# An encoder-layer kernel: the attention gates' columns join the paired product stage, two weight sums of each pair are made by adding transfers, and the last normalisation is reordered

## The chip, the core and the metric

The program runs on one core of a Trainium2 chip. Its engines are TensorE (PE: matmuls, with its weight loads shown as PEld), VectorE (DVE), ScalarE (ACT), GpSimd (POOL) and SyncE (SP), which mostly issues transfers. The metric is device time in microseconds (us) of one execution, the median over several runs; lower is better. TensorE's clock has two levels, 2.4 and 1.2 GHz; the profile gives the granted clock of a stretch as a share of the higher one.

## The reference, cut to what matters

One layer of a streaming encoder, fp32, for 512 prompt tokens and 64 sample tokens (576 in all), width 2048:

```python
ca, cb, cg, q, k, v, ag, mq, mg = split_in_proj(x @ w_in)     # 2048 -> 6144 columns
u = ca * sigmoid(cb)                                          # 8 x 128 channels
y = conv31(concat(left, u)) + conv_b                          # depthwise, 31 taps
conv_out = silu(layer_norm(y)) @ w_pw
att = chunk_attention(q, k, v, rel_table)                     # 4 heads x 128 ("self heads")
mem = memory_attention(mq, mem @ w_mem_kv)                    # 4 heads x 128 ("mem heads")
mix = concat([conv_out * silu(cg), att * silu(ag), mem * silu(mg)])
y = layer_norm(ALPHA * x + mix @ w_out)
```

The outputs are y, the new convolution state, and the new keys and values.

## The kernel before

Every fp32 product is made of three matmuls on rounded halves: a 128 x 1024 block of weights (512 KB, `wraw`) is split into `whi` (an ACT cast, L185) and `wlo` (a DVE subtraction, L186), and high*high, low*high and high*low are added up in PSUM. `stage_plan` lists the blocks in the order of their use; one block is one *stage*. `next_stage` calls `weights(i)`, which splits blocks up to two stages ahead and loads up to five ahead, from 14 buffers that raw, high and low blocks share. A stage of an ordinary column tile (`tileA`, results `accA`) is 48 matmuls of 288 columns, and a tile takes two stages.

The order of the work: the values V (`accB`), then the *product stage*, then per self head the column tiles K, Q and the gate AG, then the keys and values of the memory (16 steps over k, `mem_kv`), then per mem head the tiles MQ and MG, the upper half of the output product, the pointwise product of the convolution, and the lower half of the output product with the final layer norm.

The product stage takes column tiles in pairs. With token columns and weight rows each cut in two, a pair is computed by seven half-size products (Strassen-like) of 24 matmuls of 288 columns, instead of the 2 x 2 x 48 matmuls of two ordinary tiles. Three of the seven weight operands are raw quarters (a11, a22, a12) and four are sums (s1 to s4), made by DVE adds of 128 x 1024 (L176, L178). Results `st` go to `pos` and `neg` through ACT copies and DVE adds. There are 12 pairs: eight for the convolution's inputs and four for its gate CG, which is spilled to DRAM (`cgd`) and read back late.

Side work runs between stages. After each stage `pump(ntaps, steps)` takes `steps` steps of the generators in `side` (an attention head advances from one `yield` to the next: scores, transposes, product with V, gating) and `ntaps` taps of the convolution, one DVE instruction of 128 x 606 each (L435). The whole program's order on each engine is fixed by the order in which this code issues; the numbers that steer it are `TAP_RATE`, `TAP_RATE_KV`, `TAP_RATE_OUT` and `TAPS_OF_PRODUCT`.

A self head's steps on PE: scores (`sA` to `sD`, L695 to L698), then, after softmax on DVE and ACT (L708 to L732), transposes of the probabilities into `pt` (L737, L745; later L756 to L760), and the product with V (`so`, `sos`). For a mem head: `msc`, `mpt` (L621, L629), `mo` (L637 to L639).

The convolution's norm (`conv_ln`): column sums `mean`, squares, `var` (L892), then a diagonal of factors `dg` and its spread `ra`, `rb` (L906, L907).

At the end the last 512 output columns are computed token tile by token tile (t = 4, 0, 1, 2, 3). `settle` adds the accumulator to the residual `z` (L1086) and takes statistics; for n < 3 it also multiplies z by the gain on POOL (L1089). `finish_stats` makes row factors `lncc` on POOL (L1052 to L1062); `finish_pe` transposes them (`cT`, L1068) and makes the four corrections `t` (L1075), which DVE applies (L1078) and SP writes out.

Of the kernel before, what the change touches and what calls it, by code (L numbers as in the profile page):

```python
# [21 lines left out]
H = 4  # L22
# [16 lines left out]
TAP_RATE = 4  # L39
TAP_RATE_KV = 0  # L40
TAP_RATE_OUT = 5
TAPS_OF_PRODUCT = (1, 1, 0, 1, 1, 1, 1)
WARM = 8
CONV_PAIRS = [(C_CA + j * P, C_CB + j * P) for j in range(NCB)]
GATE_PAIRS = [(C_CG + j * P, C_CG + (j + 1) * P) for j in range(0, NCB, 2)]
PAIRS = CONV_PAIRS + GATE_PAIRS
AHEAD = 5

# [6 lines left out]
def stage_plan():  # L55
# [21 lines left out]
    for h in range(H):  # L77
        for c in (C_K, C_Q, C_AG):
            col(c + h * P)
# [30 lines left out]
def hymba_kernel(ctx: ExitStack, tc: tile.TileContext, wst, xT, memT, xp, xs, kcT, vc, mkcT, mvc, biasx,  # L110
# [47 lines left out]

    def w_load(i):
        if i < len(plan):  # L160
            for b in item_blocks(plan[i]):
                w_fetch(b)

    def w_source(it):
        if it[0] == "P":
            return w_fetch(it[1])
        n, form = it[1:]
        q = quads(PAIRS[n])
        if form[0] == "a":
            return w_fetch(q[form])  # L170
        if form == "s3":
            return sum3.pop(n)
        a21 = w_fetch(q["a21"])
        if form == "s1":
            sum3[n] = wtile("wsum")
            nc.vector.tensor_add(sum3[n], w_fetch(q["a11"]), a21)  # L176
        other = w_fetch(q[{"s1": "a22", "s2": "a11", "s4": "a12"}[form]])
        nc.vector.tensor_add(a21, a21, other)  # L178
        return a21

    def w_split(i):
        if i < len(plan) and i not in whi:
            src = w_source(plan[i])
# [5 lines left out]
    def weights(i):  # L189
        for j in range(i, i + 3):  # L190
            w_split(j)
        for j in range(i + 3, i + AHEAD + 1):
            w_load(j)
        return whi[i], wlo[i]
# [212 lines left out]
    cg_dram = [dram([P, NT], "cgd") for _ in range(NCB)]  # L407
# [8 lines left out]
    def queue_conv(j):  # L416
# [22 lines left out]
        def last():  # L439
            t = TAPS - 1  # L440
            y = t5([P, NT], "y")
# [54 lines left out]
    def gate_sink(d1, d2):  # L496
        def second(neg, b0):
# [3 lines left out]
            nc.gpsimd.dma_start(d2, neg.rearrange("p a b -> p (a b)"))  # L501

        def both(c1, neg):
            nc.scalar.activation(c1, c1, AF.Silu)
            nc.gpsimd.dma_start(d1, c1.rearrange("p a b -> p (a b)"))
        return second, both

    def strassen(sinks):
# [3 lines left out]
        for sink in sinks + [None]:  # L512
# [14 lines left out]
            if not sink:  # L527
# [17 lines left out]
             + [gate_sink(cg_dram[j], cg_dram[j + 1]) for j in range(0, NCB, 2)])  # L545
# [27 lines left out]
    def mem_attn(h, qh, ql, qs, gate_ref):  # L573
# [41 lines left out]
        yield  # L615
# [27 lines left out]
        gate = gate_ref[0]  # L643
# [32 lines left out]
    def self_attn(h, qh, ql, qs, kh, kl, k, gref):  # L676
# [102 lines left out]
        nc.tensor.matmul(os_[:, :64], vs[:64, hs], TS[:64, 256:320], start=False, stop=True)  # L779
        yield  # L780
        gate = gref[0]
# [4 lines left out]
    def self_block(h):  # L786
        k = evac2(tileA(xrhs, 2, TAP_RATE), "k")
# [6 lines left out]
        qh, ql, qs = evac_q(tileA(xrhs, 2, TAP_RATE))  # L794
        gref = [None]
        side.append(self_attn(h, qh, ql, qs, kh, kl, k, gref))
        gref[0] = evac_act(tileA(xrhs, 2, TAP_RATE), "ag", AF.Silu)
# [56 lines left out]
    def mem_block(h):  # L854
        qh, ql, qs = evac_q(tileA(xrhs, 2, TAP_RATE, 2))
        gref = [None]
        side.append(mem_attn(h, qh, ql, qs, gref))
        gref[0] = evac_act(tileA(xrhs, 2, TAP_RATE, 2), "mg", AF.Silu)
# [124 lines left out]
    for n in range(4):  # L983
        accs, sacc = tileB(mlhs2, range(4), msl, list(range(8, 16)), ntaps=TAP_RATE_OUT, before=late_mix, steps=2)
# [15 lines left out]
    def load_cg(j):  # L1000
        scg.append(t6([P, 2, HALF], "cg"))
        nc.sync.dma_start(scg[j].rearrange("p a b -> p (a b)"), cg_dram[j])
# [88 lines left out]
    def scale_g(t, n, g):  # L1091
        rows = P if t < 4 else NS_TOK
        nc.vector.tensor_mul(z[t, n][:rows], z[t, n][:rows], g[:rows])

    g = load_g(0)
    for n in range(3):
        accs, sacc = tileB(mlhs2, range(4), msl, list(range(8)))
        g2 = load_g(n + 1)
        for t in range(4):
            settle(t, n, accs[t], g)  # L1100
        settle(4, n, sacc, g)
# [20 lines left out]
    for t in (4, 0, 1, 2, 3):  # L1122
        todo = []
        for s in range(4):
            if t in (1, 2, 3) and due and (s == 3 or len(due) > 1):
                todo += finish_pe(*due.pop(0))
            part(t, s, held[s])
        settle(t, 3, accs[t], g, False)
        aggr, *rest = finish_stats(t)
        due.append((t, *rest))  # L1130
        with tc.issue_after(aggr.ins):
            for f in todo:
                f()
            scale_g(t, 3, g)
# [72 lines left out]
```

## Time and profile before

| what | value |
|---|---|
| median of 3 runs | 978.58 us (977.07 to 978.63) |
| profiled execution | 976.83 us, span 975.1 us |
| PE / DVE / ACT / POOL busy | 955.7 / 718.7 / 387.5 / 60.0 us |
| mean granted clock | 0.99 |
| V until 58.9 us, product stage until about 327 us | seven products to a pair |
| self heads until about 504 us, memory keys and values until about 545 us | |
| mem heads, upper half of the output, norm of the convolution at 740 us | |
| last matmul of the output product ends about 963.2 us | span ends at 975.1 us |

A busy PE here is a PE whose matmuls overlap each other: a row's mean duration (about 295 ns for 288 columns) is longer than the spacing of two matmuls. What a matmul costs is read from the chain of waits, as a stretch divided by its count.

### The profile page before, as it was taken

To read this page: it belongs to the slowest core of one execution; us is meant where nothing else is said; L and a number is where in the kernel's file an instruction comes from. 1 tells how busy PE (TensorE), PEld (TensorE's weight loads), DVE (VectorE), ACT (ScalarE), POOL (GpSimd) and SP (SyncE) were. 2 spreads that over 40 slices of the span, in tenths; PEclk is the share of its full clock that TensorE was granted. 3 is DMA by queue.
4 is the path that set the end of the run, shared out by engine and by line. 5 is a ranking of instruction groups with operands and counts; after the bars stand their busy time and mean duration, and the time that the engine had idled before them with its cause. 6 is when DMAs were issued, how large, how long until landed. Compare 5 with 4: busy or idle time off the path is not lost.

```text
span 975.1 us, 15245 instructions
## 1 busy us (share of the span) xinstructions
PE 955.7 (98%) x6133; PEld 881.4 (90%) x6133; DVE 718.7 (74%) x995; ACT 387.5 (40%) x667; POOL 60.0 (6%) x119
## 2 busy tenths in 40 slices
PE   9999999999999999999999999999998999999986
PEld 6899999999999999999988999989887889988864
DVE  7976998799868979898975543885988534635566
ACT  7654344443444425252537343455425313411200
POOL 0020000000000000000000000000000000012251
PEclk9999999999999999999999999999999999999987
DMA  8453333333444633333246542323354244322205
GB/s 320 143 170 113 114 104 119 127 100 101 152 138 149 231 112 124 105 101 126 78 131 191 192 137 88 111 66 110 119 193 156 75 134 135 109 80 85 76 7 187
DMA packets 44632, 124.58 MB, mean 128 GB/s; under 512 B 5710, under 2 KB 10318, under 8 KB 44562
## 3 DMA queue, kind: packets, MB, share of 16 engines
q1 hardware_dynamic: 40594, 109.88, 34.8%
q0 software_dynamic: 3680, 13.21, 3.6%
q8 instruction: 48, 0.79, 0.3%
q10 hardware_dynamic: 288, 0.52, 0.2%
q14 instruction: 22, 0.18, 0.1%
HBM read 106.72 MB, written 16.88 MB: 127 GB/s over the span
## 4 chain that ended last, share of the span: by engine, by line
PE 93%; DVE 4%; DMA 1%; ACT 1%; issue 1%; POOL 0%; DVEq 0%; SPq 0%; POOLq 0%; ACTq 0%
PE accA L234 32%; PE st L472 27%; PE accB L264 6%; PE accB L262 6%; PE accB L263 6%; PE accS L267 2%; PE accS L268 2%; PE mvacc L824 1%; PE accB L1113 1%; PE mvacc L826 1%; PE mkacc L830 1%; PE mkacc L831 1%; DVE z L1086 1%; PE mkacc L829 1%; PE accB L1114 1%
## 5 line engine op out<-in xcount | busy, mean ns | idle before, releaser
L186 DVE TENSOR_TENSOR wlo<-wraw,whi 128x1024 fp32r<-128x1024 f32 x175 | 217.7, 1247 | 175.3 <-PE accA L234 52.9
L185 ACT CAST whi<-wraw 128x1024 fp32r<-128x1024 f32 x175 | 183.2, 1050 | 296.2 <-DVE wlo L186 183.3
L234 PE MATMUL accA<-x,whi 128*128 128x288 f32 x1280 | 224.4, 297 | 0.0
L435 DVE SCALAR_TENSOR_TENSOR acc<-up,cw_sb,acc 128x606 f32<-128x606 f32 x232 | 196.6, 847 | 4.6
L234 PEld LDWEIGHTS accA<-x,whi 128*128 128x128 f32 x1280 | 187.8, 189 | 2.4 <-issue 1.5
L472 PE MATMUL st<-x,whi 128*128 128x288 f32 x768 | 153.5, 294 | 0.0
L234 PE MATMUL accA<-x,wlo 128*128 128x288 f32 x640 | 137.1, 296 | 0.0
L472 PEld LDWEIGHTS st<-x,whi 128*128 128x128 f32 x768 | 123.0, 188 | 0.3 <-ACT neg L538 0.2
L472 PE MATMUL st<-x,wlo 128*128 128x288 f32 x384 | 113.1, 295 | 0.0
L234 PEld LDWEIGHTS accA<-x,wlo 128*128 128x128 f32 x640 | 103.0, 189 | 0.0
L262 PE MATMUL accB<-whi,mix 128*128 128x512 f32 x224 | 89.1, 398 | 0.0
L264 PE MATMUL accB<-wlo,mix 128*128 128x512 f32 x224 | 88.4, 395 | 0.0
L263 PE MATMUL accB<-whi,mix 128*128 128x512 f32 x224 | 88.1, 393 | 0.0
L472 PEld LDWEIGHTS st<-x,wlo 128*128 128x128 f32 x384 | 72.0, 188 | 0.0
L472 PE MATMUL st<-t13h,wlo 128*128 128x288 f32 x192 | 56.6, 295 | 0.0
L472 PE MATMUL st<-t13l,whi 128*128 128x288 f32 x192 | 56.6, 295 | 0.0
L472 PE MATMUL st<-t13h,whi 128*128 128x288 f32 x192 | 56.5, 294 | 0.0
L264 PEld LDWEIGHTS accB<-wlo,mix 128*128 128x128 f32 x224 | 42.3, 189 | 9.8
L262 PEld LDWEIGHTS accB<-whi,mix 128*128 128x128 f32 x224 | 42.5, 190 | 9.3
L263 PEld LDWEIGHTS accB<-whi,mix 128*128 128x128 f32 x224 | 42.6, 190 | 9.2
L234 PE MATMUL accA<-sx,whi 128*128 128x288 f32 x256 | 44.5, 296 | 0.0
L178 DVE TENSOR_TENSOR wraw<-wraw,wraw 128x1024 f32<-128x1024 f32 x36 | 43.9, 1219 | 0.2
(331 smaller groups left out, 1486.0 us busy)
## 6 DMA issues: line engine op xcount, KB each, us to landing
wraw<-in_wst_dram SPq DMA_DIRECT2D x151, 512.0 KB, 3.6
xraw<-in_xT_dram SPq DMA_DIRECT2D x19, 288.0 KB, 4.5
z<-in_xp_dram SPq DMA_DIRECT2D x16, 256.0 KB, 4.6
out_y_dram<-z SPq DMA_DIRECT2D x16, 256.0 KB, 2.1
upd<-up POOLq DMA_DIRECT2D x8, 318.0 KB, 4.7
up<-upd SPq DMA_DIRECT2D x8, 318.0 KB, 4.0
yd<-y POOLq DMA_DIRECT2D x8, 288.0 KB, 2.8
y<-yd SPq DMA_DIRECT2D x8, 288.0 KB, 5.6
```

What stands on the lines that cost most here:

```text
L178: nc.vector.tensor_add(a21, a21, other)
L185: nc.scalar.copy(hi, src)
L186: nc.vector.tensor_sub(lo, src, hi.bitcast(F32))
L234: nc.tensor.matmul(acc[:, :HALF], stat[:, ws], mv[:, c], start=ki == 0 and pi == 0, stop=ki == len(klist) - 1 and pi == 2)
L262: nc.tensor.matmul(acc, lh, hi[:, ws], start=st, stop=False)
L263: nc.tensor.matmul(acc, ll, hi[:, ws], start=False, stop=False)
L264: nc.tensor.matmul(acc, lh, lo[:, ws], start=False, stop=en)
L267: nc.tensor.matmul(sacc, ss, hi[:, ws], start=st, stop=False)
L268: nc.tensor.matmul(sacc, ss, lo[:, ws], start=False, stop=en)
L435: nc.vector.scalar_tensor_tensor(acc[0], up[0][:, t:t + ACCW], cw_sb[:, j, t:t + 1], acc[0], op0=ALU.mult, op1=ALU.add)
L472: nc.tensor.matmul(acc[:, :HALF], stat[:, ws], mv, start=first and k == 0 and i == 0, stop=k == 7 and i == 2, skip_group_check=not first)
L824: nc.tensor.matmul(mvacc[t], mh[:, ts], hi[:, 512:], start=st, stop=False)
```

## The change

There are six parts.

1. The four gate tiles of the self heads (AG) leave the heads and become two more pairs of the product stage (14 pairs, 336 `st` matmuls more, 384 `accA` matmuls fewer). All gate pairs are spilled to DRAM from ACT's queue (before, from POOL's), and a self head reads its gate back after its product with V is issued.
2. Of the four weight sums of a pair, s1 and s3 are made by transfers. s3 is an ACT copy of a11 to which a POOL-issued transfer adds a21; s1 is the loaded a21 to which such a transfer adds a22. Both are started with the load of s1's stage, which now happens seven stages ahead instead of five (`AHEAD_PAIRS`). s2 and s4 stay DVE adds.
3. The taps are spread otherwise: ten to a pair instead of six, two (instead of four) after a self head's stage, one after two memory steps, three (instead of four) after a mem head's stage. The finished `y` of a channel block takes a buffer of the other pool (`t6`).
4. Each self head has four stages instead of six, with two steps of side work after each tile's stages instead of one. In the order, 48 `accA` matmuls stand between a head's scores and its first transposes (before, 96), 48 between the first and the second transposes, none between these and the product with V (before, 48). Head 3's steps lie among the memory steps, as before. A mem head loses one `yield`: the product `mo` follows `mpt` directly (before, 48 matmuls lay between).
5. In the upper half of the output product three steps are taken after a stage instead of two; `ra` comes behind nine more `accB` matmuls.
6. At the end, for n = 2 the multiplication with the gain is taken out of `settle`. POOL does it for n = 2 and for some tiles of n = 3 in the last loop, DVE for the others. `finish_pe` comes at other places: 64 `accB` matmuls stand ahead of the first `cT` (before, 40), and two tiles are finished after the last `accB` matmul (before, one).

```diff
-TAP_RATE = 4
-TAP_RATE_KV = 0
+TAP_RATE = 2
+TAP_RATE_KV = 1
+TAP_RATE_MEM = 3
...
-TAPS_OF_PRODUCT = (1, 1, 0, 1, 1, 1, 1)
+TAPS_OF_PRODUCT = (2, 1, 1, 2, 1, 1, 2)
...
-GATE_PAIRS = [(C_CG + j * P, C_CG + (j + 1) * P) for j in range(0, NCB, 2)]
+GATE_PAIRS = [(c + j * P, c + (j + 1) * P) for c, n in ((C_CG, NCB), (C_AG, H)) for j in range(0, n, 2)]
...
+AHEAD_PAIRS = 7
...
-        for c in (C_K, C_Q, C_AG):
+        for c in (C_K, C_Q):
...
+    def w_add(dst, b):
+        nc.gpsimd.dma_start(dst, wst[where[b]], accum_op=ALU.add)
+
...
-        if i < len(plan):
-            for b in item_blocks(plan[i]):
-                w_fetch(b)
+        if i >= len(plan):
+            return
+        for b in item_blocks(plan[i]):
+            w_fetch(b)
+        if plan[i][2:] == ("s1",) and plan[i][1] not in sum3:
+            n = plan[i][1]
+            q = quads(PAIRS[n])
+            sum3[n] = wtile("wsum")
+            nc.scalar.copy(sum3[n], w_fetch(q["a11"]))
+            w_add(sum3[n], q["a21"])
+            w_add(w_fetch(q["a21"]), q["a22"])
...
-            return sum3.pop(n)
+            return sum3[n]
...
-        if form == "s1":
-            sum3[n] = wtile("wsum")
-            nc.vector.tensor_add(sum3[n], w_fetch(q["a11"]), a21)
-        other = w_fetch(q[{"s1": "a22", "s2": "a11", "s4": "a12"}[form]])
-        nc.vector.tensor_add(a21, a21, other)
+        if form != "s1":
+            nc.vector.tensor_add(a21, a21, w_fetch(q[{"s2": "a11", "s4": "a12"}[form]]))
...
+            w_load(i)
...
-        for j in range(i + 3, i + AHEAD + 1):
-            w_load(j)
+        for j in range(i + 3, i + AHEAD_PAIRS + 1):
+            if j < len(plan) and (j <= i + AHEAD or plan[j][0] == "S"):
+                w_load(j)
...
-    cg_dram = [dram([P, NT], "cgd") for _ in range(NCB)]
+    gate_dram = {c: dram([P, NT], "gated") for pair in GATE_PAIRS for c in pair}
...
-            y = t5([P, NT], "y")
+            y = t6([P, NT], "y")
...
-            nc.gpsimd.dma_start(d2, neg.rearrange("p a b -> p (a b)"))
+            nc.scalar.dma_start(d2, neg.rearrange("p a b -> p (a b)"))
...
-            nc.gpsimd.dma_start(d1, c1.rearrange("p a b -> p (a b)"))
+            nc.scalar.dma_start(d1, c1.rearrange("p a b -> p (a b)"))
...
-             + [gate_sink(cg_dram[j], cg_dram[j + 1]) for j in range(0, NCB, 2)])
+             + [gate_sink(gate_dram[c], gate_dram[d]) for c, d in GATE_PAIRS])
...
-    def mem_attn(h, qh, ql, qs, gate_ref):
+    def load_gate(c):
+        g = t5([P, 2, HALF], "gate")
+        nc.sync.dma_start(g.rearrange("p a b -> p (a b)"), gate_dram[c])
+        return g
+
+    def mem_attn(h, qh, ql, qs, gref):
...
-        yield
...
-        gate = gate_ref[0]
+        gate = gref[0]
...
-    def self_attn(h, qh, ql, qs, kh, kl, k, gref):
+    def self_attn(h, qh, ql, qs, kh, kl, k):
...
-        yield
-        gate = gref[0]
+        gate = load_gate(C_AG + h * P)
+        yield
...
-        k = evac2(tileA(xrhs, 2, TAP_RATE), "k")
+        k = evac2(tileA(xrhs, 2, TAP_RATE, 2), "k")
...
-        qh, ql, qs = evac_q(tileA(xrhs, 2, TAP_RATE))
-        gref = [None]
-        side.append(self_attn(h, qh, ql, qs, kh, kl, k, gref))
-        gref[0] = evac_act(tileA(xrhs, 2, TAP_RATE), "ag", AF.Silu)
+        qh, ql, qs = evac_q(tileA(xrhs, 2, TAP_RATE, 2))
+        side.append(self_attn(h, qh, ql, qs, kh, kl, k))
...
-        qh, ql, qs = evac_q(tileA(xrhs, 2, TAP_RATE, 2))
+        qh, ql, qs = evac_q(tileA(xrhs, 2, TAP_RATE_MEM, 2))
...
-        gref[0] = evac_act(tileA(xrhs, 2, TAP_RATE, 2), "mg", AF.Silu)
+        gref[0] = evac_act(tileA(xrhs, 2, TAP_RATE_MEM, 2), "mg", AF.Silu)
...
-        accs, sacc = tileB(mlhs2, range(4), msl, list(range(8, 16)), ntaps=TAP_RATE_OUT, before=late_mix, steps=2)
+        accs, sacc = tileB(mlhs2, range(4), msl, list(range(8, 16)), ntaps=TAP_RATE_OUT, before=late_mix, steps=3)
...
-        nc.sync.dma_start(scg[j].rearrange("p a b -> p (a b)"), cg_dram[j])
+        nc.sync.dma_start(scg[j].rearrange("p a b -> p (a b)"), gate_dram[C_CG + j * P])
...
-    def scale_g(t, n, g):
-        rows = P if t < 4 else NS_TOK
-        nc.vector.tensor_mul(z[t, n][:rows], z[t, n][:rows], g[:rows])
-
...
-            settle(t, n, accs[t], g)
-        settle(4, n, sacc, g)
+            settle(t, n, accs[t], g, n < 2)
+        settle(4, n, sacc, g, n < 2)
+        gs = (g, g2)
...
-            if t in (1, 2, 3) and due and (s == 3 or len(due) > 1):
+            part(t, s, held[s])
+            if due and t > 1 and s == 2:
...
-            part(t, s, held[s])
+        if t == 1:
+            todo += finish_pe(*due.pop(0))
...
+        rows = P if t < 4 else NS_TOK
+        for n in (2, 3):
+            if t != 3 and (n == 2 or t in (4, 0)):
+                nc.gpsimd.tensor_mul(z[t, n][:rows], z[t, n][:rows], gs[n - 2][:rows])
...
-            scale_g(t, 3, g)
+            for n in (2, 3):
+                if t == 3 or (n == 3 and t in (1, 2)):
+                    nc.vector.tensor_mul(z[t, n][:rows], z[t, n][:rows], gs[n - 2][:rows])
...

```

On PE, self head 0: the last transposes of the probabilities (`pt` from `pA`, `pB`, `pS`) and what follows, before:

```order
L756 MATMUL pt_550_4190<-ident,pB_3933 128x128
L756 MATMUL pt_550_4190<-ident,pA_3932 128x128
L758 MATMUL pt_550_4190<-ident,pS_3934 128x64 x4
L760 MATMUL pt_551_4197<-ident,pS_3934 64x64
L234 MATMUL accA_4134<-x_91,whi_4047 128x288
L234 MATMUL accA_4135<-x_91,whi_4047 128x288
```

and now:

```order
L772 MATMUL pt_596_4595<-ident,pB_4412 128x128
L772 MATMUL pt_596_4595<-ident,pA_4411 128x128
L774 MATMUL pt_596_4595<-ident,pS_4413 128x64 x4
L776 MATMUL pt_597_4602<-ident,pS_4413 64x64
L789 MATMUL so_4610<-pT_583_4516,vw_4080 128x512
L790 MATMUL so_4610<-pL_584_4517,vw_4080 128x512
L791 MATMUL so_4610<-pT_583_4516,vw_4080 128x512
L789 MATMUL so_4610<-pT_586_4525,vw_4085 128x384
```

The product with V (`so`) now stands right behind the transposes, where the next column tile stood.

On PE, at the norm of the convolution, in the output product: `var` and `ra`, before:

```order
L268 MATMUL accS_7562<-wlo_7605,mixsamp_7346 128x512
L892 MATMUL var_7760<-ones,s_1051_7661 128x1 x4
L892 MATMUL var_7760<-ones,s_1051_7661 64x1
L906 MATMUL ra_7777<-dg_7771,ones 128x128 x4
L907 MATMUL rb_7778<-dg_7771,ones 128x64
L262 MATMUL accB_7813<-whi_7676,mix_7326 128x512
```

and now:

```order
L280 MATMUL accS_7806<-wlo_7697,mixsamp_7349 128x512
L906 MATMUL var_7841<-ones,s_1077_7753 128x1 x4
L906 MATMUL var_7841<-ones,s_1077_7753 64x1
L274 MATMUL accB_7802<-whi_7807,mix_7363 128x512
L275 MATMUL accB_7802<-whi_7807,mix_7363 128x512
L276 MATMUL accB_7802<-wlo_7808,mix_7363 128x512
L274 MATMUL accB_7803<-whi_7807,mix_7363 128x512
L275 MATMUL accB_7803<-whi_7807,mix_7363 128x512
L276 MATMUL accB_7803<-wlo_7808,mix_7363 128x512
L274 MATMUL accB_7804<-whi_7807,mix_7363 128x512
L275 MATMUL accB_7804<-whi_7807,mix_7363 128x512
L276 MATMUL accB_7804<-wlo_7808,mix_7363 128x512
L920 MATMUL ra_7858<-dg_7852,ones 128x128 x4
```

Nine matmuls of the output product moved between the two.

On POOL, early in the product stage (its other work there is a memset and the spill `upd` of each pair's `up`), before:

```order
L398 DMA vd_138<-v_649 64x512
L485 MEMSET up_941 128x30
L491 DMA upd_660<-up_941 128x636
L485 MEMSET up_1180 128x30
L491 DMA upd_661<-up_1180 128x636
L485 MEMSET up_1416 128x30
```

and now:

```order
L410 DMA vd_138<-v_652 64x512
L162 DMA wsum_733<-in_wst_dram 128x1024
L162 DMA wraw_729<-in_wst_dram 128x1024
L497 MEMSET up_947 128x30
L162 DMA wraw_960<-in_wst_dram 128x1024
L503 DMA upd_663<-up_947 128x636
L162 DMA wsum_964<-in_wst_dram 128x1024
L497 MEMSET up_1191 128x30
L162 DMA wsum_1208<-in_wst_dram 128x1024
L503 DMA upd_664<-up_1191 128x636
```

The rows of L162 are the adding transfers; two of them to a pair now stand among the spills in POOL's queue.

## Rows read from the trace of the kernel before

**Rows 1.** Page: engine, busy us (share) xinstructions; then the chain by engine.

```profile
PE 955.7 (98%) x6133; PEld 881.4 (90%) x6133; DVE 718.7 (74%) x995; ACT 387.5 (40%) x667; POOL 60.0 (6%) x119
...
PE 93%; DVE 4%; DMA 1%; ACT 1%; issue 1%; POOL 0%; DVEq 0%; SPq 0%; POOLq 0%; ACTq 0%
```

**Rows 2.** Waits of PE: line, releaser: us in total, times, longest.

```profile
PE cT L1068 <- POOL lncc L1056: 2.9, 1, 2.9
PE cT L1068 <- POOL lncc L1062: 2.5, 1, 2.5
PE ra L906 <- DVE dg L901: 2.5, 1, 2.5
PE mvacc L826 <- DVE ml L819: 1.5, 1, 1.5
PE mpt L621 <- ACT mp L612: 1.3, 1, 1.3
```

**Rows 3.** Chain of waits, two stretches: start us, us, what.

```profile
58.93 216.16 PE st L472 x1632
...
367.62 12.98 PE accA L234 x96
380.60 0.44 PE pt L737 x4
```

**Rows 4.** Stretches: us, busy of PE, PEld, DVE, ACT, POOL (xcount), PEclk, DMA.

```profile
193.00:215.00 22.00, 22.00 (x168) 22.00 (x167) 21.81 (x28) 8.10 (x14) 0.68 (x2) 1.00 0.36 111
```

**Rows 5.** Product stage by form: busy us, mean ns, idle before, releasers.

```profile
L186 DVE TENSOR_TENSOR wlo<-wraw,whi 128x1024 fp32r<-128x1024 f32 x71 | 86.2, 1222 | 34.5 <-PE st L472 17.7 <-ACT whi L185 16.4
L435 DVE SCALAR_TENSOR_TENSOR acc<-up,cw_sb,acc 128x606 f32<-128x606 f32 x64 | 54.2, 846 | 0.7
L178 DVE TENSOR_TENSOR wraw<-wraw,wraw 128x1024 f32<-128x1024 f32 x34 | 41.4, 1219 | 0.2
```

**Rows 6.** DMA issues: queue, count, KB each, median us to landing.

```profile
wraw<-in_wst_dram SPq DMA_DIRECT2D x151, 512.0 KB, 3.6
upd<-up POOLq DMA_DIRECT2D x8, 318.0 KB, 4.7
```

**Rows 7.** Timeline after self head 0's scores: start us, us, engine, line.

```profile
373.36 0.76 ACT L724 ACTIVATE pS<-pS,mx 64x576 f32<-64x576 f32 x1
374.03 1.23 DVE L186 TENSOR_TENSOR wlo<-wraw,whi 128x1024 fp32r<-128x1024 f32 x1
375.29 1.05 ACT L185 CAST whi<-wraw 128x1024 fp32r<-128x1024 f32 x1 [1.07 <-DVE wlo L186]
376.25 0.72 ACT L731 ACTIVATE pA<-pA,sm 128x512 f32<-128x512 f32 x1
377.67 0.49 ACT L731 ACTIVATE pB<-pB,sm 128x256 f32<-128x256 f32 x1
```

**Rows 8.** Timeline at mem head 0's transposes.

```profile
588.99 0.33 PE L629 MATMUL mpt<-ident,mps 64*128 64x64 f32 x2
590.17 0.57 ACT L624 CAST mph<-mpt 128x512 fp32r<-128x512 f32 x1
590.77 0.69 DVE L625 TENSOR_TENSOR mpl<-mpt,mph 128x512 fp32r<-128x512 f32 x1 [0.81 <-ACT mph L624]
```

**Rows 9.** Timeline of PE at three places, then DVE at the end.

```profile
745.82 0.63 PE L263 MATMUL accB<-whi,mix 128*128 128x512 f32 x1
747.10 0.63 PE L263 MATMUL accB<-whi,mix 128*128 128x512 f32 x1
...
939.39 0.63 PE L1114 MATMUL accB<-whi,mix 128*128 128x512 f32 x1
941.96 0.59 PE L1114 MATMUL accB<-whi,mix 128*128 128x512 f32 x1
...
963.28 0.69 DVE L1086 TENSOR_TENSOR z<-accB,z 128x512 f32<-128x512 f32 x1 [2.11 <-PE accB L1115]
964.91 2.65 DVE L1078 SCALAR_TENSOR_TENSOR z<-z,lnmv,t 128x512 f32<-128x512 f32 x4
```

## The prediction

> **What bounds the kernel now.** I read the page's busy times and its chain by engine first, then PE's waits, then the chain in two stretches for the price of a matmul, then single places. PE is busy 955.7 us and is 93% of the chain that ended last [rows 1]; only five of its waits are above 1.2 us, together 10.7 us [rows 2]. So the time is PE's work plus its few stalls. In the product stage DVE is nearly as full: 21.81 of 22 us, with PE busy for all 22 [rows 4]. The reader should see two different covers. In the product stage DVE has almost no room, and PE still never waits. In the heads DVE and ACT have room, but a softmax is a chain, hidden by the matmuls that stand between its steps. The change takes matmuls from the second place.
>
> **The change part by part.** All sums are made against the profiled execution, 976.83 us (1.7 us around its span of 975.1), which is 1.75 us under the median of 978.58.
>
> *PE's own work.* A product matmul costs 216.16/1632 = 0.1325 us, an attention-stage matmul 12.98/96 = 0.1352 us [rows 3]. 336 are added (44.5 us) and 384 go (51.9 us): -7.4 us. This is the only work removed from PE.
>
> *Weight sums.* DVE loses 20 adds of 1219 ns in all, s1 and s3 of 12 pairs against two more pairs of two, and gets more taps to a pair. A convolution pair now holds seven splits (8.6), two adds (2.4), three result adds of half the size of a 128x1024 add or less (1.8 at most), ten taps (8.5) and about 1 us of inputs: 22.3 us or a little less [rows 5], against 168 x 0.1325 = 22.25 us of PE. That is as full as before, when PE had no wait [rows 4]; I take 0. From the other side: where it is over by 5% for eight pairs, 9 us.
> The adding transfers are not in this trace. A plain 512 KB load takes 3.6 us, a POOL-issued 318 KB spill 4.7 [rows 6]. Worked from these, an adding transfer takes between 3.6 us and, at the spill's rate and with its destination read as well, 2 x 4.7 x 512/318 = 15.1 us. It is started about six stages before its sum is split, 6 x 24 x 0.1325 = 19 us. Hence 0, and I take the value near the spill, 7.6 us; at the upper end it still fits, with 4 us left for a plain load. What hides it is that lead; without it each pair would pay the excess.
> On this path the rows show POOL's spill landing within 4.7 us while DVE is 99% busy [rows 4, 6], and PE without a wait. The Trainium skill ("SBUF — State Buffer", SBUF: two separate sides, the "DVE blocks DMA" trap) says that a transfer issued from GpSimd's queue can be starved of its descriptors while VectorE holds the port the two share. By that rule 28 more transfers from this queue are the risk of the change, and it is the third rival below. The trace agrees with it only so far that POOL's spill is slower for its size than SP's load.
>
> *Self heads.* In head 0 the scores end at 367.62. Now 48 matmuls follow, not 96, so PE asks for the scaled probabilities at 367.62 + 48 x 0.1352 = 374.1. DVE's split runs from 374.03, and it waits for the end of those same 48 matmuls; ACT's weight cast waits for it, 375.29 to 376.3; only then come the scales, the last needed one ending at 377.67 + 0.49 = 378.2 [rows 7]. The order on ACT and DVE is the same after the change (exponentials, cast, scales; split, reciprocal), and what covered it was 96 matmuls, to 380.60 [rows 3]. Cost 4.0 us. In head 1 the reciprocal stands ahead of the split and no cast is between; the scales take 376.25 to 378.16 = 1.9 us after exponentials that end at 374.1 [rows 7], or about 1 us earlier since no taps are there: between 0.9 and 2.2, I take 1.2. In head 2 several tap instructions and a split stand ahead of the reciprocal: between 1.2 and 4.2 us, I take 3.0, nearer to head 0, whose order it shares. The product with V now follows the second transposes at once; six of its matmuls use the first transposes, so only the copy of the second can be late: 0 to 0.6 us a head, taken 0.3. Sum: 9.1 us.
>
> *Memory keys and values.* Before, their start waited 1.5 us for DVE, which had head 3's softmax in hand [rows 2]. That softmax now comes four steps later: -1.5 us. But DVE then has taps ahead of the first operands: from 0 to four taps and a split, 4 x 0.846 + 1.222 = 4.6 us [rows 5]. I take 0, since a whole softmax ahead of the operand cost only 1.5 us before.
>
> *Mem heads.* The transposes end at 588.99 + 0.33 = 589.3; the last low part ends at 590.77 + 0.69 = 591.5 [rows 8]. Four of the six `mo` matmuls fit between (0.94 us at 0.235, which is 0.1325 x 512/288), so 1.2 us is bare where ACT's weight cast stands between the two copies (heads 0 and 1), about half that in the other two: 3.6 us in sum; bounds 0 and 4.8. One tap less in each stage lets ACT's scales come earlier, and of the old wait of 1.3 us at `mpt` [rows 2] I count 0.8 as gone.
>
> *Norm of the convolution.* Nine matmuls (9 x 0.235 = 2.1 us) now stand in the wait of 2.5 us [rows 2]: -2.1. Behind that wait PE ran at its lower clock: from 745.82 to 747.10 a 512-column matmul took 0.43 us [rows 9]. Six such at 0.19 us too much: -1.2.
>
> *The end.* The first `cT` waited 2.9 us [rows 2]; 24 more matmuls (5.6 us) now stand ahead of it: -2.9. Eight matmuls behind it ran at 0.43 us, (941.96 - 939.39)/6 [rows 9]: -1.5. A second stretch of this kind later, behind eight small matmuls, I count half: -0.8. Against it, after the last matmul two tiles are finished instead of one: four more corrections, 2.65 us [rows 9]; `cT`'s own wait of 2.5 us [rows 2] stays. Balance -2.6 us. The gain's multiplications on POOL lie beside matmuls.
>
> *Sum.* Gains 7.4 + 1.5 + 0.8 + 3.3 + 2.6 = 15.6; losses 9.1 + 3.6 = 12.7; balance -2.9: 973.9 us for the profiled execution, 975.7 us as a median. So four fifths of the gain are given back in the heads.
>
> **The rivals.**
> *The covers hold.* The chains of the heads may run earlier than on before's clock, since DVE has no taps in heads 0 and 1 and ACT no gate and fewer table loads. For: DVE waits for PE at these places already [rows 7]. Against: it is this wait for PE that doesn't move. If 2 us of stalls are left, 965 us.
> *The heads' stalls whole, and the clock with them.* All at their upper bounds: head 1 +1.0, head 2 +1.2, products with V +0.9, mem heads +1.2, memory start +4.6 = 8.9 us more, and a low-clock stretch of 1.5 us behind the three longest. The trace has such stretches behind waits of 2.5 and 2.9 us and none behind those of 1.3 and 1.5 us [rows 2, 9]; head 0's 4.0 is longer than either. Together 989; a likely part of it, 983. This is the slower side: it decides once the stalls of the heads exceed 12.7 + 4.9 = 17.6 us.
> *The product stage slips.* POOL's adding transfers or DVE's 22.3 us a pair come last there. From 1 us a pair it costs 14 us: 990 or more. Against: the lead of 19 us.
> *Nothing of note.* The gate read-back or POOL's gain multiplications eat the small balance: 977 to 980.
>
> **How the numbers follow.** The forecast has 0.42, and its own range is 971 to 980.5; the covers hold 0.20; the stalls whole 0.27; the product stage 0.07; nothing of note 0.04. What a measurement of this kernel can tell from no change is 0.2%, 2 us, so faster is below 976.6 and slower above 980.5. Faster: 0.24 of the forecast's 0.42 plus 0.20 = 0.44. Within: 0.15 + 0.04 = 0.19. Slower: 0.03 + 0.27 + 0.07 = 0.37. The range of 8 in 10 goes from 965 to 988, over most of both rivals.
>
> **What would show it.** PE's busy time falls by some 7 us if the first term is right. PE's waits should list the first transposes of heads 0 and 2 (3 to 4 us each, on ACT's scales), `mo` on DVE's or ACT's copies, and no longer `ra` or the first `cT`. The product stage should end close to two pairs later, 44.5 us, with no wait of `st`. The time after the last matmul of the output product should grow from 12 to about 14.5 us. The forecast is wrong if the heads show no waits, if `st` waits for `wsum`, or if the clock falls in the heads.

## The result, and the profile after

The changed kernel takes 995.81 us (994.32 to 997.06, 4 runs) beside 977.83 us of the kernel before on the same chip: a ratio of 1.0179, 95% interval 1.0167 to 1.0191. It is slower by 18 us, where I had forecast 975.7 us in a range of 965 to 988. Its span is 994.1 us against 975.1, at a mean clock of 0.984.

The page of the changed kernel, busy times (compare [rows 1]) and transfers issued by POOL (compare [rows 6]; queue, count, KB each, median us to landing):

```profile
PE 957.4 (96%) x6085; PEld 878.5 (88%) x6085; DVE 700.0 (70%) x986; ACT 402.4 (40%) x685; POOL 81.1 (8%) x140
...
wsum<-in_wst_dram POOLq DMA_DIRECT2D x14, 512.0 KB, 8.2
wraw<-in_wst_dram POOLq DMA_DIRECT2D x14, 512.0 KB, 6.9
...
upd<-up POOLq DMA_DIRECT2D x8, 318.0 KB, 7.4
```

PE's busy time has not fallen by 7 us, though 48 matmuls are gone; it has risen by 1.7 us. The adding transfers (`wsum`, and `wraw` on POOL's queue) land after 8.2 and 6.9 us, close to the 7.6 I had taken. The page's chain of waits covers little of this execution, so I go by PE's waits and by stretches instead.

PE's waits after the change, to compare with [rows 2] (line, releaser: us in total, times, longest; some short ones and those ahead of the product stage are left out):

```profile
PE mvacc L838 <- ACT mh L832: 5.1, 2, 4.6
PE pt L753 <- ACT pA L747: 4.9, 2, 3.6
PE pt L753 <- issue: 3.7, 1, 3.7
PE mo L654 <- DVE mpl L641: 2.0, 6, 0.7
PE st L484 <- ACT neg L550: 1.8, 2, 1.1
PE mpt L637 <- ACT mp L629: 1.3, 1, 1.3
PE pt L776 <- DVE pL L767: 1.3, 1, 1.3
PE ra L920 <- DVE dg L915: 1.1, 1, 1.1
PE pt L772 <- DVE pL L757: 1.0, 1, 1.0
PE cT L1082 <- POOL lncc L1076: 0.2, 1, 0.2
```

The first wait of `cT` (2.9) and more than half of that of `ra` are gone, as forecast; so is nearly all of the last `cT`'s (2.5), which I had kept in the sum. New are `pt` in the self heads (3.7, 3.6, 1.3 us in heads 0, 2 and 1, and 2.3 us in head 3), `mo` and `st`; the wait at the first memory step (`mvacc`) has grown from 1.5 to 4.6 us.

Head 0's wait as a timeline (start us, us, engine, line; the last number is the engine's idle time before):

```profile
417.01 1.23 DVE L197 TENSOR_TENSOR wlo<-wraw,whi 128x1024 fp32r<-128x1024 f32 x1 [3.51 <-PE accA L246]
418.26 1.04 ACT L196 CAST whi<-wraw 128x1024 fp32r<-128x1024 f32 x1 [1.68 <-DVE wlo L197]
419.21 0.72 ACT L747 ACTIVATE pA<-pA,sm 128x512 f32<-128x512 f32 x1
420.83 0.30 PE L753 MATMUL pt<-ident,pA 128*128 128x128 f32 x1 [3.65 <-issue]
```

The split (L197) begins when the 48 matmuls end, ACT's weight cast follows it, and only then come the scales (L747) that the transposes need.

Now both kernels by stretch: product stage; self heads with memory keys and values; mem heads up to the end of their last `mpt`. (The memory steps of the kernel before end at 560.3 us, not at about 545 as the table ahead of the prediction has it.) Columns are length, busy time (and instructions) of PE, PEld, DVE, ACT and POOL, then granted clock, DMA share and GB/s. Before:

```profile
58.90:327.10 268.20, 268.20 (x2025) 268.01 (x2024) 226.31 (x259) 116.65 (x182) 14.82 (x35) 1.00 0.42 138
327.10:560.30 233.20, 231.40 (x1647) 220.68 (x1646) 189.97 (x280) 97.79 (x180) 6.21 (x15) 1.00 0.40 129
560.30:684.70 124.40, 123.08 (x895) 117.83 (x893) 74.04 (x111) 59.39 (x127) 2.38 (x5) 1.00 0.32 101
```

and after:

```profile
59.50:376.50 317.00, 313.91 (x2362) 312.79 (x2361) 277.60 (x335) 150.71 (x225) 35.44 (x56) 1.00 0.65 181
376.50:579.70 203.20, 187.08 (x1263) 174.08 (x1262) 123.27 (x197) 76.97 (x154) 4.08 (x10) 0.97 0.39 125
579.70:711.25 131.55, 127.85 (x895) 120.39 (x893) 70.58 (x104) 59.45 (x127) 1.79 (x4) 0.97 0.29 94
```

The length minus PE's busy time is PE's idle time; what is left is work at the granted clock. The whole account of the 19.0 us of span, with the estimates of the prediction in the last column (the fourth row also holds the upper half of the output and the convolution's norm):

| stretch | before | after | change | forecast |
|---|---|---|---|---|
| up to the product stage | 58.9 | 59.5 | +0.6 | 0 |
| product stage | 268.2 | 317.0 | +48.8 | +44.5 |
| self heads, memory keys and values | 233.2 | 203.2 | -30.0 | -44.3 |
| mem heads to the lower half of the output | 289.0 | 293.6 | +4.6 | -0.5 |
| lower half to its last matmul, then to the end | 125.8 | 120.8 | -5.0 | -2.6 |

From the self heads and memory steps, 51.9 us of matmuls left. PE's idle time there rose from 1.8 to 16.1 us, and its busy time is 187.1 us; in the repaired kernels below the same work takes 181.1 to 181.4. So nearly 6 us of the loss is the clock. In the mem heads PE's idle time rose from 1.3 to 3.7 us and its busy time by 4.8; about 3 of these are the clock, which was at its lower level for 6.8 us (below).

Six places after the change, same columns:

```profile
421.90:430.10 8.20, 8.20 (x53) 8.16 (x51) 2.60 (x5) 1.86 (x4) 0.54 (x1) 0.79 0.10 38
450.00:456.60 6.60, 6.60 (x49) 6.39 (x48) 3.33 (x11) 3.34 (x11) 0.15 (x1) 1.00 0.12 47
497.00:505.10 8.10, 8.10 (x52) 8.10 (x50) 7.91 (x12) 1.81 (x4) 0.54 (x1) 0.79 0.10 38
515.70:525.20 9.50, 4.92 (x19) 4.34 (x20) 8.76 (x15) 3.31 (x10) 0.00 (x0) 0.64 0.70 217
553.30:557.30 4.00, 3.71 (x22) 3.25 (x23) 2.68 (x7) 1.80 (x6) 0.00 (x0) 1.00 0.12 20
644.00:650.80 6.80, 6.41 (x25) 6.22 (x26) 6.66 (x11) 1.20 (x3) 0.00 (x0) 0.50 0.25 80
```

Behind the waits of 3.6 us in heads 0 and 2 the granted clock is 0.79, and the 48 matmuls that take 6.5 us elsewhere take 8.2. Behind head 1's 1.3 us it is 1.00. At the first memory step it is 0.64. In the mem heads (head 1) it is 0.50 over 6.8 us, though PE's waits ahead of that are only 0.3, 0.7 and 0.4 us, within 3 us.

### The profile page after: what moved, and what is told of

It is laid out like the page before. It is cut to its first block, busy times and chain, and to the rows that moved or that the text cites. A ratio compares the mean times of both kernels' runs of the same rounds, so it can differ in the third digit from the quotient of the medians.

```text
span 994.1 us, 15242 instructions
## 1 busy us (share of the span) xinstructions
PE 957.4 (96%) x6085; PEld 878.5 (88%) x6085; DVE 700.0 (70%) x986; ACT 402.4 (40%) x685; POOL 81.1 (8%) x140
## 5 line engine op out<-in xcount | busy, mean ns | idle before, releaser
L197 DVE TENSOR_TENSOR wlo<-wraw,whi 128x1024 fp32r<-128x1024 f32 x179 | 222.1, 1246 | 185.4 <-PE accA L246 54.4
L246 PE MATMUL accA<-x,whi 128*128 128x288 f32 x1024 | 183.3, 302 | 0.0
L484 PE MATMUL st<-x,whi 128*128 128x288 f32 x896 | 179.4, 295 | 2.4 <-ACT neg L550 1.8
L246 PEld LDWEIGHTS accA<-x,whi 128*128 128x128 f32 x1024 | 154.2, 193 | 1.9 <-issue 1.5
L484 PEld LDWEIGHTS st<-x,whi 128*128 128x128 f32 x896 | 143.4, 188 | 3.4 <-ACT neg L550 2.5
L484 PE MATMUL st<-x,wlo 128*128 128x288 f32 x448 | 131.9, 295 | 0.0
L246 PE MATMUL accA<-x,wlo 128*128 128x288 f32 x512 | 111.4, 300 | 0.0
L246 PEld LDWEIGHTS accA<-x,wlo 128*128 128x128 f32 x512 | 84.2, 193 | 0.0
L484 PEld LDWEIGHTS st<-x,wlo 128*128 128x128 f32 x448 | 84.0, 188 | 0.0
L484 PE MATMUL st<-t13h,whi 128*128 128x288 f32 x224 | 66.0, 295 | 0.7 <-ACT pos L545 0.7
L484 PE MATMUL st<-t,whi 128*128 128x288 f32 x224 | 45.0, 295 | 0.0
```

Of the source, the lines that this page charges most:

```text
L197: nc.vector.tensor_sub(lo, src, hi.bitcast(F32))
L246: nc.tensor.matmul(acc[:, :HALF], stat[:, ws], mv[:, c], start=ki == 0 and pi == 0, stop=ki == len(klist) - 1 and pi == 2)
L484: nc.tensor.matmul(acc[:, :HALF], stat[:, ws], mv, start=first and k == 0 and i == 0, stop=k == 7 and i == 2, skip_group_check=not first)
```

## The experiments

Times are medians; where a ratio to the kernel before stands, its 95% interval is beside it. "The changed kernel" is the one of the diff.

**The new end alone** (e1_end_only): the kernel before with the last loop of the changed one and `steps=3`.

```
 (the kernel before)
+            settle(t, n, accs[t], g, n < 2)     # and the new last loop, word for word
...
-        ... before=late_mix, steps=2)
+        ... before=late_mix, steps=3)
```

> The kernel before with only the new end and three side steps in the upper half of the output product. Theory A (the new end is a gain by itself, since the first cT finds its factors made and PE keeps its clock; what is lost is lost in the heads): the wait of 2.9 us at the first cT goes, so do the two stretches at the low clock behind it, and two finishes after the last matmul cost 2.5 us; together 4 to 6 us less than before, 972 to 974 us. The wait at ra stays, since here no matmuls come between it and var. Rival (the end only gains in the changed kernel because its work there was moved in from elsewhere): within 1 us of before, 977 to 979 us.

972.34 us beside 978.34, ratio 0.9949 (0.9933 to 0.9966). As theory A has it: the end is a gain by itself, 6 us, and the loss is elsewhere. Two of its waits:

```profile
PE ra L906 <- DVE dg L901: 2.5, 1, 2.5
PE cT L1068 <- POOL lncc L1062: 0.7, 1, 0.7
```

Of `cT`'s waits of 2.9 and 2.5 us [rows 2] 0.7 us is left, since the last tile's factors are made while the other tile is finished, and `ra` keeps its 2.5, since here no matmuls stand between it and `var`: `steps=3` alone does not bring the nine matmuls of the changed kernel there. Which other part of the change does was not tested.

**The first memory tiles loaded early** (e2_mem_early), ahead of head 3's Q tile instead of at the start of the memory steps. In the changed kernel the first memory step waits like this (start us, us, engine, line; SPq is SP's queue):

```profile
515.60 0.65 ACT L680 CAST qh<-accA 128x256 fp32r<-128x256 f32 x2 [8.13 <-PE accA L246]
515.72 0.33 SPq L158 DMA_DIRECT2D wraw<-in_wst_dram  x1
516.10 2.32 SPq L819 DMA_DIRECT2D mraw<-in_memT_dram  x5
519.82 1.13 ACT L832 CAST mh<-mraw 128x256 fp32r<-128x256 f32 x3 [1.81 <-DMA mraw<-in_memT_dram]
520.28 0.79 PE L838 MATMUL mvacc<-whi,mh 128*128 128x512 f32 x1 [4.58 <-ACT mh L832]
```

The memory loads (`mraw`, L819) stand in SP's queue behind a weight load (L158) which waits until 515.7 for PE to end the last Q stage; the tile lands at 519.8, and only then is it split (`mh`).

```
+        if h == H - 1:                 # ahead of head 3's Q tile
+            for kk in range(3):
+                load_mem(kk)
```

> The changed kernel with the first three memory tiles loaded before head 3's Q tile, ahead of the weight load that waits for PE in SP's queue. Theory A (the 4.6 us wait at the first memory step is a place in a queue: the loads stand behind a weight load that waits for the last Q stage): the wait goes to under 0.5 us and the low-clock stretch behind it too, 5 to 7 us less than the changed kernel, 989 to 991 us. Rival (DVE's taps or ACT's casts are late there anyway, as I had bounded it): the wait stays above 3 us with another releaser, 994 to 996 us.

995.11 us: not measurably less than the changed kernel (two runs). The wait fell only from 4.6 to 2.7 us, and the stretch of heads and memory steps from 203.2 to 201.2 us. Behind the 2.7 us the clock stayed at 1.00 (517.8 to 524.6 us), but it fell later, behind head 3's waits. Theory A was half right: the load was one of two things in a row. ACT now (e2_mem_early, same view):

```profile
515.02 0.65 ACT L680 CAST qh<-accA 128x256 fp32r<-128x256 f32 x2 [8.13 <-PE accA L246]
516.22 1.04 ACT L196 CAST whi<-wraw 128x1024 fp32r<-128x1024 f32 x1 [0.55 <-DVE wlo L197]
517.17 0.27 ACT L682 COPY qs<-accA 128x32 f32<-128x32 f32 x2
517.33 1.03 ACT L833 CAST mh<-mraw 128x256 fp32r<-128x256 f32 x3
```

With the tile there, `mh` (L833) still comes behind the evacuation of the Q tile (L680, L682) and a weight cast, all of which wait for the end of the same Q stage.

**Memory tiles loaded and split early** (e8_kv_ready): as before, and the first two splits are issued there too.

```
+            split_mem(0)               # mh and ml of the first two tiles
+            split_mem(1)
```

> The changed kernel with the first memory tiles loaded, and the first two of them split, before head 3's Q tile. Theory A (the wait at the first memory step has two layers, a load behind a weight load in SP's queue and behind it ACT's order, where the split stands behind the evacuation of the Q tile): the 4.6 us wait goes to under 0.5 us and PE keeps its clock there, 4 to 7 us less, 989 to 992 us. Rival (the time won is lost again at head 3's softmax inside the memory steps): the wait goes but the memory steps end less than 2 us earlier, 994 us or more.

988.83 us, 7 us less than the changed kernel; the wait is gone, and the stretch of heads and memory steps shrinks from 203.2 to 195.7 us. So the wait had two layers, and only taking both away removes it.

**The mem heads' yield back** (e3_mem_yield):

```
         nc.scalar.activation(pss[:64], pss[:64], AF.Copy, scale=sm[:64, 4:5])
         yield
+        yield
         pT = []
```

> The changed kernel with the mem heads' second yield back, so that 48 matmuls stand between mpt and mo again. Theory A (mo directly behind mpt is bare and lets the clock fall): the waits of mo (2.7 us) go and the mem heads, from the end of the memory keys to the last product, become 6 to 9 us shorter, 987 to 990 us in all. Rival (the mem heads grew because the taps of the side work shifted): the waits go but less than 3 us is won, 993 us or more.

988.94 us, 6.9 less, within what theory A gave. No wait of `mo` is left, and the stretch up to the end of the last `mpt` is 124.4 us, as before the change; of the 7.2 us that it lost, about 3 are the clock, which stays at 1.00.

**All four sums by DVE again** (e6_dve_sums): no adding transfers, 14 pairs, the new tap numbers. `s1` and `s3` are DVE adds as before the change.

```
-            w_add(sum3[n], q["a21"])
-            w_add(w_fetch(q["a21"]), q["a22"])
...
+            nc.vector.tensor_add(sum3[n], w_fetch(q["a11"]), a21)
+        nc.vector.tensor_add(a21, a21, w_fetch(q[{"s1": "a22", "s2": "a11", "s4": "a12"}[form]]))
```

> The changed kernel with all four weight sums of a pair as DVE adds again, no adding transfers; 14 pairs and the new tap numbers stay. Theory A (the adding transfers are in time, and DVE is the full engine of the product stage): DVE gets 2 x 1.22 us a pair more, which does not fit beside ten taps, so the product stage becomes up to 2.4 us a pair longer, 10 to 30 us, 1005 to 1025 us. Rival (the transfers are what makes the product stage 4 us longer than its matmuls): the stage shrinks to 44.5 us over that of before and the time falls to 990 to 992 us.

991.17 us, 4.6 less than the changed kernel. Theory A was wrong. The rival's time came, but only in part for its reason. The product stage with 28 more DVE adds, the mem heads up to the last `mpt`, and the spill that POOL issues:

```profile
59.70:373.80 314.10, 313.05 (x2362) 312.59 (x2361) 299.09 (x353) 138.47 (x209) 12.50 (x30) 1.00 0.41 139
576.50:705.10 128.60, 124.90 (x895) 117.56 (x893) 70.56 (x104) 59.42 (x127) 2.16 (x4) 1.00 0.31 96
...
upd<-up POOLq DMA_DIRECT2D x8, 318.0 KB, 2.8
```

The product stage is 2.9 us shorter than with the transfers (317.0). DVE is busy for 299 of 314 us and PE is idle for 1 us instead of 3: a DVE at 95% over the whole stage does not bound it. The mem heads are 2.9 us shorter too (131.55 in the changed kernel), though their code and their waits of `mo` are the same (2.0 us in six waits again): here the clock stayed at 1.00. So of the 6.2 us between the two profiled executions about 3 are the transfers, and about 3 are a fall of the clock that came in one and not in the other. What a late transfer costs is seen at the second pair's, issued while the first pair is computed (changed kernel; timeline):

```profile
66.16 0.88 POOL L162 DMA_DIRECT2D wraw<-in_wst_dram  x1 [0.23 <-issue]
78.32 1.05 ACT L196 CAST whi<-wraw 128x1024 fp32r<-128x1024 f32 x1 [4.99 <-DMA wraw<-in_wst_dram]
79.27 0.39 ACT L550 COPY neg<-st 128x288 f32<-128x288 f32 x1
79.72 0.53 PE L484 MATMUL st<-x,whi 128*128 128x288 f32 x2 [1.11 <-ACT neg L550]
```

POOL issues the adding transfer at 66.2; ACT's cast of its block waits 5.0 us for it until 78.3, and the copy of a result (`neg`, L550), which has nothing to do with it, stands behind in ACT's queue. PE waits for that copy.

**Steps of the self heads spaced** (e7_spaced): two steps after a head's first stage, one, one and two after the others, instead of two after each.

```
-        k = evac2(tileA(xrhs, 2, TAP_RATE, 2), "k")
+        k = evac2(tileA(xrhs, 2, TAP_RATE, (2, 1)), "k")
-        qh, ql, qs = evac_q(tileA(xrhs, 2, TAP_RATE, 2))
+        qh, ql, qs = evac_q(tileA(xrhs, 2, TAP_RATE, (1, 2)))
```

> The changed kernel with the self heads' steps spaced 2, 1, 1, 2 over a head's four stages instead of 2, 2, 2, 2: 96 matmuls stand between the scores and the first transposes again, with no matmul added. Theory A (the loss in the self heads is the cover that was cut from 96 to 48 matmuls, and the clock that falls behind the two long waits): the waits at pt of heads 0 to 2 (8.5 us) go, so do two low-clock stretches of 1.6 us, and the product with V covers part of the wait at the first memory step: 11 to 15 us less than the changed kernel, 981 to 985 us. Rival (the heads are late because DVE and ACT have too much in them with the gates read back): the waits move to other places and less than 5 us is won, 991 us or more.

976.24 us, ratio to before 0.9986 (0.9974 to 0.9999): 19.6 us less than the changed kernel, more than theory A gave. The stretch of heads and memory steps:

```profile
375.50:559.70 184.20, 181.44 (x1262) 169.50 (x1261) 123.25 (x199) 77.88 (x156) 4.05 (x11) 1.00 0.43 138
```

184.2 us instead of 203.2, at a clock of 1.00; PE's idle time falls from 16.1 to 2.8 us. That is nearly the 181.3 that 233.2 minus 51.9 gives. I had counted the waits of heads 0 to 2, their low clock, and part of the wait at the first memory step. The last product with V now stands right ahead of that step and covers nearly all of it (its wait is 0.8 us), so the low clock behind it goes as well, about 2 us, and head 3's waits at `pt` fall from 2.3 to 1.0 us. The mem heads, not repaired here, still take 131.4 us.

**A wait filled with matmuls** (e9_filler): 12 matmuls on zeros ahead of the first transposes of heads 0 and 2. They add nothing to any result.

```
+        for _ in range(12 if h in (0, 2) else 0):
+            nc.tensor.matmul(b0, warm[:, :P], warm, start=True, stop=True)
```

> The changed kernel with 12 matmuls on zeros (2.7 us at the high clock) issued ahead of the first transposes of heads 0 and 2, where PE otherwise waits 3.6 us; they compute nothing that is used. Theory A (PE's clock falls because PE stands still, and the low stretch behind it is a cost of its own): with the wait filled the 48 matmuls behind take 6.5 us instead of 8.2 in both heads, the transposes start at the same time, and the total is 3 us less, 992 to 993.5 us. Rival (the stretch behind the wait is slow for another reason, such as weights that come late): it stays at 8 us, and the time is the same or up to 1 us more.

993.98 us, 1.8 less, which two runs do not set apart from noise; the stretches decide. The two stretches behind the filled waits, and one in the memory steps:

```profile
421.40:428.00 6.60, 6.60 (x52) 6.57 (x50) 2.58 (x5) 1.79 (x4) 0.54 (x1) 1.00 0.12 47
494.90:501.50 6.60, 6.60 (x52) 6.57 (x50) 6.49 (x10) 1.81 (x4) 0.54 (x1) 1.00 0.13 47
550.00:554.00 4.00, 3.53 (x11) 2.96 (x11) 1.98 (x6) 1.97 (x7) 0.00 (x0) 0.50 0.08 27
```

The same 48 matmuls take 6.6 us at a clock of 1.00, where they took 8.2 at 0.79. So the clock's fall is a cost of its own, 1.6 us for each such wait, and follows from PE standing still. Part of the 3.2 us was lost again in head 3: behind its waits at `pt` (1.0 and 1.3 us, as in the changed kernel) the clock now fell to 0.50, where the changed kernel kept 1.00 (553.3 to 557.3 above).

**The short cover alone** (e13_before_48): the kernel before with two side steps after each self-head stage instead of one; 12 pairs, and nothing else changed.

```
-        k = evac2(tileA(xrhs, 2, TAP_RATE), "k")          # and the same for q and ag
+        k = evac2(tileA(xrhs, 2, TAP_RATE, 2), "k")
```

> The kernel before with two side steps after each of the self heads' stages instead of one, and nothing else: 48 matmuls between a head's scores and its first transposes, none between the second transposes and the product with V, still 12 pairs. Theory A (the cover between a head's steps is the cause by itself): pt waits 2 to 4 us in each of heads 0 to 2, the clock falls behind the long waits, and the kernel is 8 to 13 us slower than before, 986 to 991 us. Rival (the short cover hurts only together with the moved gates, taps and loads): under 4 us slower, 982 us or less.

1006.66 us, ratio 1.0292 (1.0272 to 1.0313): 28 us slower, much more than theory A gave. Its waits at `pt`, and the 48 matmuls behind head 0's wait:

```profile
PE pt L737 <- ACT pA L731: 11.3, 3, 3.9
PE pt L737 <- issue: 3.9, 1, 3.9
```

```profile
374.60:383.00 8.40, 8.40 (x52) 8.40 (x50) 7.20 (x10) 2.66 (x5) 0.00 (x0) 0.76 0.00 0
```

All four heads wait nearly 4 us, and the clock falls to 0.76 behind head 0's wait. The spacing of the steps alone loses more than the whole change did.

**All repairs** (e10_all): the spaced steps, the early memory tiles, the yield and the DVE sums together on the changed kernel.

> The changed kernel with four repairs together: the heads' steps spaced 2, 1, 1, 2, the first memory tiles ready, the mem heads' second yield back, and all weight sums as DVE adds. Theory A (these four account for the loss, and what is left are the 48 matmuls saved and the new end): 995.8 - 13 - 3 - 7 - 4.5 = 968 us, range 965 to 972, faster than before and faster than the kernel before with the new end alone (972.3). Rival (14 pairs cost something of their own in the heads, such as the gates' reads or DVE's taps): 975 us or more.

963.32 us (963.17 to 964.53), ratio 0.9858 (0.9842 to 0.9875): 1.4% faster than before, and faster than with the new end alone. That is below theory A's range of 965 to 972: I had put the spacing in with 13 us, and e7 gave 19.6. Heads with memory steps, and mem heads:

```profile
373.40:554.80 181.40, 181.10 (x1262) 169.19 (x1261) 128.16 (x205) 77.94 (x156) 3.83 (x10) 1.00 0.43 141
554.80:679.40 124.60, 123.28 (x897) 118.00 (x895) 70.37 (x104) 59.59 (x127) 2.15 (x4) 1.00 0.30 99
```

**Three repairs, adding transfers kept** (e11_all_adding).

> The changed kernel with three of the four repairs: steps spaced 2, 1, 1, 2, the first memory tiles ready, the mem heads' second yield back; the adding transfers stay. Theory A (the adding transfers cost their own 3 to 4 us in the product stage, through late blocks in ACT's queue): 966 to 968 us, 0.3 to 0.5% above the kernel with all four repairs (963.3), with waits of st on ACT's copies. Rival (the repaired heads leave the transfers free of cost): within 1.5 us of 963.3.

969.58 us (966.25 to 971.16), ratio 0.9906 (0.9881 to 0.9931): 6 us above the kernel with all repairs, more than either theory gave and with more scatter. Its waits in the product stage, and a place in the mem heads:

```profile
PE st L484 <- ACT neg L550: 4.2, 2, 3.6
```

```profile
653.20:656.50 3.30, 3.30 (x14) 2.86 (x14) 1.87 (x4) 3.20 (x6) 0.00 (x0) 0.50 0.58 159
```

The product stage is 4.8 us longer than with all repairs (319.2 against 314.4 us): the waits and, behind the long one, a stretch at the low clock. Another 1.5 us lie in the mem heads, where the clock fell behind the wait of 1.3 us at `mpt`; in the kernel with all repairs it stayed at 1.00 behind the same wait. So of the 6.8 us between the two profiled executions the transfers explain about 5.

## Why the prediction was wrong

The step that failed is the price of the clock in the heads: the sum put it at nothing, and the runs show about 9 us. The start of the memory steps failed beside it, by 4.8 us. Of what I had named as signs of a wrong forecast, the clock falling in the heads came. Term by term:

- *PE's own work, -7.4 us*: right. With all repairs (e10) the heads with the memory steps take 181.4 us, and 233.2 - 51.9 is 181.3; e6's product stage of 314.1 us is 45.9 us longer than before for 44.5 us of matmuls.
- *Self heads, +9.1 us*: the waits were right, 3.7, 1.3 and 3.6 us against 4.0, 1.2 and 3.0, and in head 0 for the reason given (the cast that waits for the split, ahead of the scales). The 0.9 us for the products with V did not show. Head 3's steps I had not priced at all: its transposes wait 2.3 us among the memory steps.
- *Memory keys and values, -1.5 us, with 0 taken of 0 to 4.6*: this is a failed term. The first step waited 4.6 us, all waits there rose from 1.8 to 5.1, and not for taps: a load behind a weight load in SP's queue, and behind that the split in ACT's queue. I had bounded it by DVE's work and never asked when the transfer was issued. That my upper bound reads 4.6 too is chance.
- *The clock*: the step that failed most. I took what the clock gives back at the norm and at the end (1.2, 1.5 and 0.8 us), and put what it costs in the heads only into a rival, though my own row of the waits of 2.5 and 2.9 us said what waits of 3.6 us would do. Nearly 6 us in the heads with the memory steps and about 3 in the mem heads are lost to it. With them and the 4.8 us of the term above, the sum is a loss of 11 us instead of a gain of 2.9. The 3 us in the mem heads are partly luck: of six profiled executions with `mo` right behind `mpt` five show a fall there, e6 none.
- *Mem heads, +3.6 and -0.8 us*: the waits sum to 2.7 us and the old one of 1.3 stays; the low clock over the next tile (0.50 over 6.8 us in head 1) was not in the sum.
- *Weight sums, 0*: the landing time was right as a median, the lead was not. By the code a transfer is started five stages ahead of its split (seven less the two of the split), 16 us and not 19. For the second pair even that was not there: POOL issues in order and stood until 58.1 us ahead of V's spills, so the transfer went out at 66.2 and took 12.1 us. It is 2.9 us in the stage by e6, 4.8 by e11. My doubt that DVE's 22.3 us a pair would bound the stage was wrong: with two more adds it got shorter. [rows 4] are one full stretch of 22 us; over the whole stage before, DVE was busy for 226.3 of 268.2 us. The rule of the Trainium skill ("SBUF — State Buffer", SBUF: two separate sides, the "DVE blocks DMA" trap) would have VectorE, while it runs an operation in a two-port mode, keep GpSimd from writing a transfer's descriptors. A busy VectorE alone does not do that here: with it busy for 299 of 314 us the spill `upd` landed in 2.8 us (e6), before in 4.7, beside the adding transfers in 7.4. In which mode its operations ran the traces don't show. Whether the transfers were slowed by the traffic (DMA share 0.65 in the stage, before 0.42) or in the queue, these runs don't tell.
- *Norm and end, -5.9 us*: right in kind. The norm's `ra` kept 1.1 us of its wait, where I had left 0.4. The end gave -5.0 against -2.6, and 6 us alone in e1. Behind the last matmul of the output product 14.4 us pass, before 11.8, as forecast: the last `cT` starts 3.6 us after that matmul in both kernels, and PE only does the other tile's matmuls meanwhile. So the wait that went there gained nothing. The excess lies ahead of that matmul, where 106.4 us stand against 114.0: two stretches at the low clock cost 1.7 us each before, not 1.5 and 0.8, and one tile's finish moved behind the last matmul.
- The slower rival had the mechanism, the places and the price of the clock (983 to 989 us), and got 0.27 of the chance. Its sum still missed head 3, the mem heads' clock and the transfers.

What stays open: how much of the transfers' cost is their traffic and how much their lateness, and what decides whether the clock falls behind waits of about 1 us, since with the same code and waits it did in some executions and not in others.

## What to carry to other kernels

Moving matmuls out of a stage also moves the cover of whatever chain runs beside them; check, for each chain of the stage, that the matmuls left between its steps still last longer than the chain, and space the steps before judging the move (four numbers here were worth 20 us). Price a wait of TensorE with the low-clock stretch behind it, and look at that stretch's clock in both kernels before crediting an edit with a few microseconds. Where an operand comes late, follow it through every queue in turn, the transfer's issue first: removing one layer of two gained 2 us in the stretch, removing both 7.5.

## What the runs showed of the hardware that I had not expected

- Behind idle stretches of 3.6 us of PE the granted clock was 0.79 over the next 8 us; with the idle time filled by matmuls on zeros it stayed at 1.00.
- Behind shorter waits it differed: 1.00 behind head 1's 1.3 us and behind 2.7 us in e2, but 0.50 behind 1.3 us at `mpt` in e11 and behind three waits of 0.3 to 0.7 us in the changed kernel.
- A VectorE busy for 299 of 314 us left PE idle for 1 us only, and a 318 KB spill issued by POOL beside it landed in 2.8 us (median).
- A 512 KB transfer that adds, issued by POOL, took 5.2 to 12.1 us to land (median 7.6), a plain load of this size 3.7.
